# Laying out the first mixer's small operands and weights on the host instead of turning them on the chip

## The chip, the cores and the metric

The kernel runs on one core of a Trainium2 chip. The metric is the device time of one execution in microseconds, the median of several runs; lower is better. Arranging the input arrays on the host is not part of that time.

## What is computed

A block of two layers on 256 tokens of width 1024 (a conditioned mixer with a causal convolution, then a mixture of 32 experts, two per token), and behind it a second block of attention and feed-forward layers. The change touches the first block's mixers only, the first one above all:

```python
c_act = silu(c)
mods = (c_act @ ada_w[i] + ada_b[i])          # sh_m, sc_m, g_m, sh_f, sc_f, g_f
h = x * (1.0 + sc_m) + sh_m
# layer 0: conformer_conv
a, g = split(h @ w_in + b_in, 2)
u = a * sigmoid(g)
u = causal_depthwise_conv(u, w_dw) + b_dw     # 31 taps per channel
u = silu(layer_norm(u, ln_g, ln_b))
y = u @ w_out + b_out
# layer 1: short_gated_conv
gb, gc, v = split(h @ w_in, 3)
y = (gb * causal_depthwise_conv(gc * v, w_dw)) @ w_out    # 3 taps
# both: x = layer_norm(ALPHA * x + (1 + g_m) * y), then the mixture of experts
```

## The kernel before

The whole program is written under a manual schedule, each instruction with its engine: the text of the Python program is the order in which each engine gets its work.

**The stream of weights** (class `Stream`). All weights of both blocks go through one stream of units of up to 1 MB, loaded by SyncE (SP). There are 11 slots of 8 KB per partition, and 4 more lent during the first block. `pump` emits loads as long as slots are free, keeping one back; so the first `pump(0)`, inside `first_consts`, emits 14 units: `m` and `k` in the order m0 m1 k0 k1 m2 m3 k2 k3 m4 m5 k4 k5 m6 m7. Loads of later units are emitted where `done` or a split gives a slot back, so on SP they stand behind everything that was written before. Units of kind `k` and `i3` are split into two half-precision parts before use: ACT makes the high part (L120), VectorE the low one (L107). Behind k6 and k7 come i3 (two units), then a02 (four units for the modulation vectors g of layer 0), and so on to the experts.

**The start** (`first_consts`, L405). SP loads c, `ada_b`, x and then the units of `pump(0)`; behind them the 31 x 1024 tap matrix `wd` (L422), the rows `vq` and `vb`, and eight loads of the routers' weights and biases. TensorE turns `ada_b` (16 small transposes, L456 and L457) and x (16 transposes, L467, copied out by ACT, L468) so that channels lie on partitions. Two closures, `taps` and `vectors`, are kept for later.

**The first mixer's loop** (`first_mixer`, L711). For n = 0 to 3: `modulation(n)` multiplies two `m` units by c (L727), copies the result out as `adar` (L732), turns it (L735), sums it on VectorE into `c4` (L737), adds the bias `vb0` (L739), modulates two blocks of x (L574, L576, L580, L581: `mf`, `xh`, `xl`) and splits k(2n) and k(2n+1). Row block k multiplies one split unit by x (L752). The order is: the matmuls of `modulation(n)`, row block 2n-1 with the transposes of L735 inside, the rest of `modulation(n)`, for n = 2 `taps` and for n = 3 `vectors`, row block 2n; behind the loop the split of i3 and row block 7.

`taps` turns the 31 taps into what the convolution needs: 160 small matmuls (L478) and three transposes (L482) on TensorE, two copies on VectorE (`w4`, `taps`), and `m32`. `vectors` makes `vqT` (eight transposes, L495, one copy, L497), the scaled biases `ba` (L500, L501) and the routers' joined weights (L504, L505).

**The convolution.** Gates on ACT and VectorE use `vqT` and `ba`; GpSimd clears the borders of the tiles `U` (L787, L788) and builds diagonals from `m32` and `w4` (`diag`, L823); TensorE does five of eight channel blocks, VectorE the three in `VECTOR_Q` with `taps` as scalars (L795). M02 (L538) is the first step of that stage, product 6 (L777) the next.

Tiles of the pool `ch` (c8, `wd`, the routers' staging tiles, `c4`, `mf`) and of the pool `cv` (`sig`, `U`, `diag`, `V`) use the same memory one after the other; a tile of `cv` waits for the last reader of what lay there. Both blocks' later stages are not touched, except that layer 1's gated mixer takes its input weights and small vectors from the new arrays.

## Time and profile before

| | us |
|---|---|
| median of 3 runs (2452.61 to 2458.95) | 2457.27 |
| profiled execution, its own time | 2455.99 |
| span of the profiled execution | 2454.3 |
| TensorE busy | 2345.2 |
| VectorE busy | 1227.5 |
| ACT busy | 897.1 |
| GpSimd busy | 107.4 |

The span counts from the first to the last instruction. Instructions of one engine are listed with the line that issued them; L12 is line 12 of the kernel before. An idle time in square brackets is the time the engine stood still ahead of the instruction, with what ended it as far as the profile can tell; where an instruction waits for several things, the one named is the last by the profile's events, and can be a wrong one. Matmuls overlap, so the duration of a merged row of them counts from the first to the last. The TensorE clock is given as a share of the full rate. DMA rates are those of the core's 16 DMA engines together.

### The profile page before, as it was taken

What the parts mean: (1) busy time and instruction counts of PE and PEld (TensorE: products, weight loads), DVE (VectorE), ACT (ScalarE), POOL (GpSimd) and SP (SyncE); (2) the same over time, 40 slices, a digit from 0 to 9 for tenths busy, and PEclk for the clock granted to TensorE, in tenths of its full rate; (3) what the DMA queues carried; (4) which work ended last, traced back from release to release, by engine and by line L of the source; (5) the groups of instructions that cost most, each with busy time, mean ns of one, the idle gap of its engine ahead of it and who ended that gap; (6) DMA issues with size and microseconds to landing.
All of it is one profiled execution on the core that took longest, in us unless ns stands there. A gap on an engine that the chain in (4) does not pass through costs nothing.

```text
span 2454.3 us, 38061 instructions
## 1 busy us (share of the span) xinstructions
PE 2345.2 (96%) x16219; PEld 1383.2 (56%) x16219; DVE 1227.5 (50%) x1910; ACT 897.1 (37%) x1222; POOL 107.4 (4%) x169
## 2 busy tenths in 40 slices
PE   7989999999999999999979999999999999999998
PEld 5534343443386443334448855547888875554985
DVE  2775122111277222111157486968557567877654
ACT  2342111111143211111134447675444445676442
POOL 0100000000000000000020011110000002110000
PEclk8999999999999999999999999999999999999999
DMA  8977999999998999999976544536656555445651
GB/s 273 405 317 318 421 421 421 421 421 421 414 362 322 377 420 421 421 421 421 420 296 228 173 168 172 189 138 231 216 172 241 197 173 176 139 160 183 246 167 67
DMA packets 191033, 709.91 MB, mean 289 GB/s; under 512 B 15054, under 2 KB 50382, under 8 KB 134026
## 3 DMA queue, kind: packets, MB, share of 16 engines
q1 hardware_dynamic: 187850, 698.50, 73.7%
q10 hardware_dynamic: 3008, 8.92, 1.1%
q8 instruction: 129, 2.11, 0.3%
q14 instruction: 46, 0.38, 0.0%
HBM read 706.33 MB, written 1.05 MB: 288 GB/s over the span
## 4 chain that ended last, share of the span: by engine, by line
PE 50%; DMA 8%; issue 4%; DVE 4%; ACT 1%; POOL 0%; ACTq 0%; DVEq 0%; SPq 0%; POOLq 0%
PE ps L1470 18%; PE ps L1592 9%; PE ps L1198 6%; PE acc L1450 5%; DMA w<-in_e_w_up 3%; DMA w<-in_e_w_gate 3%; PE acc L1431 3%; PE ps L1220 2%; DVE w L107 1%; DMA w<-in_e_w_down 1%; PE acc L1692 1%; PE ps L1152 1%; PE ps L1954 1%; PE acc L1840 1%; PE acc L1236 1%
## 5 line engine op out<-in xcount | busy, mean ns | idle before, releaser
L107 DVE SCALAR_TENSOR_TENSOR w<-w,w 128x2048 f16<-128x2048 f32 (+3 forms) x239 | 525.6, 2213 | 234.8 <-ACT w L120 234.4
L120 ACT ACTIVATE w<-w 128x2048 f16<-128x2048 f32 (+3 forms) x239 | 434.6, 1832 | 251.5 <-PE ps L1470 140.0
L1470 PEld LDWEIGHTS <-w 128*128 128x128 f16 x4992 | 461.2, 112 | 11.4 <-issue 2.0
L1470 PE MATMUL ps<-xh,w 128*128 128x256 f16 (+1 forms) x3328 | 378.5, 257 | 1.1 <-DVE w L107 1.0
L1252 DVE SCALAR_TENSOR_TENSOR hid<-ps,ws,sil 128x512 f32<-128x512 f32 x32 | 24.0, 751 | 476.1 <-PE ps L1198 476.1
L1198 PE MATMUL ps<-w,xl 128*64 128x512 f32 x1024 | 240.4, 599 | 15.7 <-DMA w<-in_e_w_gate 15.6
L1198 PE MATMUL ps<-w,xh 128*64 128x512 f32 x1024 | 238.9, 595 | 14.8 <-DMA w<-in_e_w_gate 12.1
L1220 PE MATMUL ps<-w,hT 128*64 128x512 f32 x1024 | 237.0, 596 | 7.1 <-DMA w<-in_e_w_down 4.0
L1470 PE MATMUL ps<-xl,w 128*128 128x256 f16 (+1 forms) x1664 | 222.9, 257 | 1.9 <-DVE xl L333 1.9
L1592 PE MATMUL ps<-w,xh 128*128 128x512 f16 (+2 forms) x896 | 195.3, 362 | 0.5 <-ACT xh L332 0.5
L1198 PEld LDWEIGHTS ps<-w,xh 128*64 128x64 f32 x1024 | 80.0, 137 | 156.8 <-issue 121.2
L1198 PEld LDWEIGHTS ps<-w,xl 128*64 128x64 f32 x1024 | 78.4, 137 | 158.8 <-issue 120.1
L1220 PEld LDWEIGHTS ps<-w,hT 128*64 128x64 f32 x1024 | 80.3, 137 | 139.1 <-issue 111.0
L1227 ACT ACTIVATE yh<-y 128x512 f16<-128x512 f32 x64 | 40.3, 630 | 259.7 <-DVE y L1226 259.7
L1592 PEld LDWEIGHTS <-xh 128*128 128x128 f16 x896 | 85.4, 98 | 85.6 <-issue 2.4
L1226 DVE TENSOR_TENSOR y<-ps,g 128x512 f32<-128x512 f32 x64 | 44.0, 688 | 169.7 <-PE ps L1220 169.7
L1208 ACT ACTIVATE hT<-ps 128x512 f32<-128x512 f32 x32 | 19.1, 597 | 272.2 <-PE ps L1206 272.2
L1450 PE MATMUL acc<-w,hh 128*128 128x512 f16 x384 | 114.2, 379 | 0.0
L1592 PE MATMUL ps<-w,xl 128*128 128x512 f16 (+2 forms) x448 | 106.1, 362 | 0.0
L1431 PE MATMUL acc<-w,hh 128*128 128x512 f16 x320 | 95.2, 379 | 0.0
L1450 PE MATMUL acc<-w,hl 128*128 128x512 f16 x192 | 72.8, 379 | 0.0
L1592 PEld LDWEIGHTS <-xl 128*128 128x128 f16 x448 | 43.5, 98 | 45.7
(392 smaller groups left out, 2853.5 us busy)
## 6 DMA issues: line engine op xcount, KB each, us to landing
w<-in_e_w_gate SPq DMA_DIRECT2D x128, 1024.0 KB
w<-in_e_w_up SPq DMA_DIRECT2D x128, 1024.0 KB
w<-in_e_w_down SPq DMA_DIRECT2D x128, 1024.0 KB
w<-in_ffn_in SPq DMA_DIRECT2D x80, 1024.0 KB
w<-in_w_in SPq DMA_DIRECT2D x50, 1024.0 KB
w<-in_ffn_out SPq DMA_DIRECT2D x44, 1024.0 KB
w<-in_ada_w SPq DMA_DIRECT2D x40, 1024.0 KB
w<-in_b_w_in SPq DMA_DIRECT2D x12, 1024.0 KB
```

Of the source, the lines that this page charges most:

```text
L107: self.nc.vector.scalar_tensor_tensor(h[:, 1, :n], t[:, :n], WS, h[:, 0, :n], op0=OP.mult, op1=OP.subtract)
L120: self.nc.scalar.activation(h[:, 0, :n], t[:, :n], AF.Copy, scale=WS)
L1152: nc.tensor.matmul(pt[:, e * P : e * P + P], t[:, c, k + e :: 8], o[:, c], start=(i == c == 0), stop=(i == c == 1))
L1198: nc.tensor.matmul(pt[64 * e : 64 * e + 64], XT[j][:, 4 * h + k, 64 * e : 64 * e + 64], W[e][:, k * 512 : k * 512 + 512], start=(h == 0 an ...
L1220: nc.tensor.matmul(banks[n][64 * e : 64 * e + 64], hT[j][:, 2 * h + i, 64 * e : 64 * e + 64], W[e][:, i * D + n * 512 : i * D + n * 512 + ...
L1226: nc.vector.tensor_mul(y[:, sl], banks[n], G[:, sl])
L1227: nc.scalar.activation(yh[:, sl], y[:, sl], AF.Copy, scale=XS)
L1236: nc.tensor.matmul(accs[c][n], t, y[:, n * 512 : n * 512 + 512], start=False, stop=(j == 15 and i == 1), skip_group_check=True)
L1431: nc.tensor.matmul(accs[c][n], H[tx][:, 2 * h + f, c * P : c * P + P], ho[:, tw, f * D + n * 512 : f * D + n * 512 + 512], start=(j == 0 a ...
L1450: nc.tensor.matmul(accs[c][n], H[tx][:, 2 * h + f, c * P : c * P + P], ho[:, tw, f * D + n * 512 : f * D + n * 512 + 512], start=(j == 0 a ...
L1470: nc.tensor.matmul(pt[:, f % 2 * S + t0 : f % 2 * S + t1], h[:, tw, k * n + f : (k + 1) * n : nf], X[tx][:, 4 * (q % 2) + k, t0:t1], start ...
L1592: nc.tensor.matmul(pt[:, :n], X[tx][:, nk * q + k, c * P : c * P + P], h[:, tw, k * n : k * n + n], start=(q == 0 and k == 0 and tx == tw ...
```

## The change

Arrays are arranged on the host by `layouts` so that what one load brings lies in the order in which it is used: x by channel (`lay_x`), c with layer 0's two modulation biases (`lay_c`), one array per kind of unit in which each partition's part of a unit is contiguous (`lay_m`, `lay_k`, `lay_t` for i3, `lay_b` for layer 1's input weights), one array `lay_f` with `vbT`, `vqT`, `lnT` and the routers' weights side by side, and one, `lay_w`, with both forms of the taps. The transposes, the tap matmuls and the copies behind them are dropped; `taps` and `vectors` are no more. x by channel is loaded from ACT's queue; x by token is still loaded, behind the small rows. `ba` and `m32` are made at the end of `first_consts`.

The diff, with `first_units`' address arithmetic and the removed closures cut:

```diff
         def head(k):
             if k % 2 == 0:
-                src = a["ada_w"]
                 for h in range(2):
-                    m = [(dap(src, 4 * h * 6 * D + j * D + 128 * k, [[8 * 6 * D, P], [6 * D, 4], [1, 256]]), 256 * j, 256 * j + 256)
-                         for j in range(2)]
-                    u.setdefault("m", []).append(w.add(m, (4, 512), False))
-            u.setdefault("k", []).append(w.add([(dap(a["a_w_in"], 128 * k * 2 * D, [[2 * D, P], [D, 2], [1, 768]]), None, None)], (2, 768)))
+                    u.setdefault("m", []).append(block("lay_m", k + h, (4, 512), False))
+            u.setdefault("k", []).append(block("lay_k", k, (2, 768)))
...
+        def block(t, i, shape, split=True):
+            n = shape[0] * shape[1]
+            return w.add([(dap(a[t], i * P * n, [[n, P], [shape[1], shape[0]], [1, shape[1]]]), None, None)], shape, split)
...
     def first_consts(self, pool, early, keep, xT):
-        c8 = early.tile([P, 8], F32, name="c8")
-        vb = pool.tile([40, D], F32, name="vb")
-        vq = vb[32:]
-        wd = early.tile([31, D], F32, name="wd")
+        c8 = early.tile([P, 24], F32, name="c8")
+        vb = pool.tile([21, D], F32, name="vb")
+        fix = pool.tile([P, 768], F32, name="fix")
...
-        nc.sync.dma_start(c8, a["c"].rearrange("b (p k) -> p (b k)", p=P))
-        rows(nc.sync, vb[:12], self.ROWS_B[:1])
+        nc.sync.dma_start(c8, a["lay_c"])
+        nc.scalar.dma_start(xT, a["lay_x"])
+        self.w.pump(0)
+        t = keep.tile([P, 32 * 5 + 31 * 3], F32, name="taps")
+        nc.sync.dma_start(fix, a["lay_f"])
+        nc.sync.dma_start(t, a["lay_w"])
+        rows(nc.sync, vb, self.ROWS_B)
         nc.sync.dma_start(self.x, a["x"].rearrange("b (c p) d -> p (b c) d", p=P))
-        self.w.pump(0)
-        nc.sync.dma_start(wd, dap(a["a_w_dw"], 0, [[D, 31], [1, D]]))
-        rows(nc.sync, vq, self.ROWS_Q)
-        rows(nc.sync, vb[12:21], self.ROWS_B[1:])
         ca = self.ca = pool.tile([P, 8], F32, name="ca")
-        nc.scalar.activation(ca, c8, AF.Silu)
+        nc.scalar.activation(ca, c8[:, :8], AF.Silu)
+        self.w4 = t[:, : 32 * 5]
+        self.taps = {q: t[:, 160 + 31 * n : 191 + 31 * n] for n, q in enumerate(VECTOR_Q)}
+        self.vbT = fix[:, :96].rearrange("p (k r) -> p k r", k=8)
+        self.vqT = fix[:, 96:160].rearrange("p (k r) -> p k r", k=8)
+        self.lnT = fix[:, 160:192].rearrange("p (i l k) -> p i l k", i=2, l=2)
...
+            self.rw.append((fix[:, 192 + 288 * l : 480 + 288 * l].rearrange("p (k n) -> p k n", k=8), b))
...
         self.vb0 = pool.tile([P, 2, 8], F32, name="vb0")
         for j in range(2):
-            nc.vector.tensor_scalar(self.vb0[:, j], pt[:, 96 + j : 112 : 2], float(j), XS, op0=OP.add, op1=OP.mult)
+            nc.vector.tensor_scalar(self.vb0[:, j], c8[:, 8 + 8 * j : 16 + 8 * j], float(j), XS, op0=OP.add, op1=OP.mult)
...
+        m32 = self.m32 = keep.tile([P, 32], F32, name="m32")
+        nc.vector.tensor_reduce(m32, self.ident.rearrange("p (r j) -> p j r", r=4), axis=AX.X, op=OP.add)
+
+        self.ba = pool.tile([P, 8, 2], F32, name="ba")
+        for j in range(2):
+            nc.vector.tensor_scalar(self.ba[:, :, j], self.vqT[:, :, 2 * j], 1.0 / INV, None, op0=OP.mult)
...
     def first_mixer(self, pool, zp):
-                consts = list(self.first_consts(pool, mp, keep, z))
+                self.first_consts(pool, mp, keep, z)
...
                     next(m, None)
-                    if n > 1:
-                        consts.pop(0)(cb)
                     rows(2 * n)
```

`layouts` computes the arrays on the host by reshaping and transposing, for example:

```python
out["lay_x"] = v["x"][0].T.reshape(8, P, S).transpose(1, 0, 2)
w0 = v["ada_w"][0].reshape(P, 2, 4, 6, 4, 256)[:, :, :, :2]
out["lay_m"] = w0.transpose(4, 1, 0, 2, 3, 5)
wk = v["a_w_in"][0].reshape(8, P, 2, D)
out["lay_k"], out["lay_t"] = wk[..., :768], wk[..., 768:].transpose(2, 1, 0, 3)
```

## Rows read from the trace of the kernel before

**Rows 1.** The page, part 1: engine, busy us (share of the span), instructions.

```profile
PE 2345.2 (96%) x16219; PEld 1383.2 (56%) x16219; DVE 1227.5 (50%) x1910; ACT 897.1 (37%) x1222; POOL 107.4 (4%) x169
```

**Rows 2.** Stretches: length, busy us by engine (instructions), TensorE clock, DMA share, GB/s.

```profile
15.60:26.00 10.40, 6.01 (x37) 4.13 (x36) 4.96 (x6) 4.08 (x4) 0.00 (x0) 0.67 1.07 370
...
26.00:38.60 12.60, 10.69 (x97) 7.71 (x100) 4.96 (x6) 4.69 (x5) 0.00 (x0) 1.00 1.07 367
...
47.60:55.60 8.00, 7.95 (x161) 7.96 (x161) 1.76 (x1) 1.11 (x1) 0.00 (x0) 0.51 0.23 52
...
71.40:76.80 5.40, 5.37 (x34) 4.21 (x35) 2.71 (x8) 1.48 (x1) 1.08 (x3) 0.68 1.03 410
...
186.00:192.00 6.00, 6.00 (x42) 2.97 (x41) 4.04 (x16) 1.87 (x2) 0.00 (x0) 1.00 0.00 0
```

**Rows 3.** Order of time of SP's queue: start, duration, line, operation, count.

```profile
36.00 0.94 SPq L422 DMA_DIRECT2D wd<-in_a_w_dw  x1
...
52.80 4.50 SPq L93 DMA_DIRECT2D w<-in_a_w_in  x4
```

**Rows 4.** Order of time, TensorE's instructions: start, duration, line, operation, idle before.

```profile
13.20 1.06 PE L727 MATMUL ps<-w,ca 128*32 128x512 f32 x8 [1.60 <-DMA w<-in_ada_w]
...
26.03 1.92 PE L727 MATMUL ps<-w,ca 128*32 128x512 f32 x16
...
38.55 1.92 PE L727 MATMUL ps<-w,ca 128*32 128x512 f32 x16
...
47.65 8.00 PE L478 MATMUL ps<-ident,wd 31*32 31x8 f32 x160 [2.70 <-DMA wd<-in_a_w_dw]
...
62.72 1.92 PE L727 MATMUL ps<-w,ca 128*32 128x512 f32 x16
...
69.05 1.12 PE L495 MATMUL ps<-ident,vb 8*128 8x8 f32 x8
...
80.84 3.64 PE L538 MATMUL ps<-w,ca 128*32 128x512 f32 x32
...
86.48 0.27 PE L777 MATMUL ps<-xh,w 128*128 128x256 f16 x1 [2.00 <-DVE U L789]
```

**Rows 5.** Order of time, VectorE alone.

```profile
15.66 0.17 DVE L737 TENSOR_REDUCE c<-ps 128x4 f32<-128x16 f32 x1 [9.94 <-PE ps L735]
...
69.61 1.76 DVE L107 SCALAR_TENSOR_TENSOR w<-w,w 128x1536 f16<-128x1536 f32 x1 [0.68 <-ACT w L120]
...
72.92 1.76 DVE L107 SCALAR_TENSOR_TENSOR w<-w,w 128x1536 f16<-128x1536 f32 x1 [1.55 <-ACT w L120]
...
74.59 0.22 DVE L497 COPY vqT<-ps 128x64 f32<-128x64 f32 x1
...
78.96 2.81 DVE L107 SCALAR_TENSOR_TENSOR w<-w,w 128x2048 f16<-128x2048 f32 x1 [3.30 <-ACT w L120]
...
83.75 2.29 DVE L107 SCALAR_TENSOR_TENSOR w<-w,w 128x2048 f16<-128x2048 f32 x1 [1.98 <-ACT w L120]
```

**Rows 6.** Order of time, GpSimd alone.

```profile
68.99 0.13 POOL L787 MEMSET U<- 128x30 f32 x1 [12.62 <-DMA w<-in_ada_w]
...
75.72 0.12 POOL L787 MEMSET U<- 128x30 f32 x1 [6.29 <-DVE rw L505]
...
75.84 3.79 POOL L823 TENSOR_TENSOR diag<-m,w 128x1024 f32<-128x1024 f32 x2
```

**Rows 7.** DMA views: rate in 0.15 us slices (0:6), packets in 48:54, 300:312.

```profile
GB/s 0 0 0 0 0 0 0 0 0 0 0 0 12 15 1 164 164 0 55 109 27 0 55 0 27 328 273 355 382 437 437 328 382 410 437 437 382 437 437 437
...
DMA packets 1214, 0.36 MB, mean 59 GB/s; under 512 B 950, under 2 KB 1206, under 8 KB 1213
...
DMA packets 695, 5.06 MB, mean 422 GB/s; under 512 B 78, under 2 KB 78, under 8 KB 78
```

**Rows 8.** Waits of TensorE, 60 to 232 us, longest first: total, times, longest.

```profile
PE ps L556 <- DVE col L557: 4.8, 2, 2.5
```

**Rows 9.** Waits of all engines, 600 to 820 us: TensorE's longest for a load.

```profile
PEld ps L1220 <- DMA w<-in_e_w_down: 3.7, 3, 2.2
```

More of the change, by code (lines that the diff above doesn't have):

```diff
@@ L31 @@
 NEG = -1.0e30
+VECTOR_Q = (0, 2, 4)
 LOW = 2.0 ** 11
@@ L347 @@
     )
-    VECTOR_Q = (0, 2, 4)
     AFTER = ("F N G H", "S S F S N G S S")
@@ L386, in first_units @@
                 elif nm[0] == "i" and l == 0:
-                    u[nm] = [w.add([(dap(a["a_w_in"], j * D + 768, [[2 * D, P], [128 * 2 * D, 8], [1, 256]]), None, None)], (8, 256))
-                             for j in range(2)]
+                    u[nm] = [block("lay_t", j, (8, 256)) for j in range(2)]
                 elif nm[0] == "i":
-                    u[nm] = [cols(a["b_w_in"], 3 * D, j * D + 256 * int(nm[1]), nm != "i0") for j in (1, 2, 0)]
+                    u[nm] = [block("lay_b", 3 * int(nm[1]) + j, (8, 256), nm != "i0") for j in (1, 2, 0)]
                 elif nm == "o":
@@ L460, in first_consts @@
         for j in range(2):
-            nc.vector.tensor_scalar(self.vb0[:, j], pt[:, 96 + j : 112 : 2], float(j), XS, op0=OP.add, op1=OP.mult)
-        for k in range(0, 8, 2):
-            px = self.acc()
-            for e in range(2):
-                for c in range(2):
-                    o = e * S + c * P
-                    nc.tensor.transpose(px[:, o : o + P], self.x[:, c, (k + e) * P : (k + e) * P + P], self.ident)
-            nc.scalar.activation(xT[:, k : k + 2].rearrange("p k t -> p (k t)"), px, AF.Copy)
@@ L470, in taps @@
-        def taps(pt):
-            pq = [q for q in range(8) if q not in self.VECTOR_Q]
-            for r in range(4):
-                for n, q in enumerate(pq):
-                    for s in range(4):
-                        c0 = 256 * (q // 2) + 64 * s + q % 2
-                        nc.tensor.matmul(pt[32 * r : 32 * r + 32, (4 * n + s) * 8 : (4 * n + s) * 8 + 8], wd[:, c0 : c0 + 63 : 2],
-                                         self.ident[:31, r:32:4], start=True, stop=True, tile_position=(0, 32 * r))
-            for n, q in enumerate(self.VECTOR_Q):
-                c0 = 256 * (q // 2) + q % 2
-                nc.tensor.transpose(pt[:, 256 + 31 * n : 287 + 31 * n], wd[:, c0 : c0 + 255 : 2], self.ident[:31, :31])
-            w4 = self.w4 = keep.tile([P, 32 * len(pq)], F32, name="w4")
-            nc.vector.tensor_copy(w4, pt[:, : 32 * len(pq)])
-            t = keep.tile([P, 31 * len(self.VECTOR_Q)], F32, name="taps")
-            nc.vector.tensor_copy(t, pt[:, 256 : 256 + 31 * len(self.VECTOR_Q)])
-            self.taps = {q: t[:, 31 * n : 31 * n + 31] for n, q in enumerate(self.VECTOR_Q)}
-            m32 = self.m32 = keep.tile([P, 32], F32, name="m32")
-            nc.vector.tensor_reduce(m32, self.ident.rearrange("p (r j) -> p j r", r=4), axis=AX.X, op=OP.add)
@@ L818, in first_mixer @@
                     gate(q, out[q])
-                on = [q for q in range(8) if q not in self.VECTOR_Q]
+                on = [q for q in range(8) if q not in VECTOR_Q]
                 def diagonals(n):
@@ new lines, with layouts @@
+    "r_b_expert", "e_w_gate", "e_w_up", "e_w_down", "positions_2", "w_in_2", "sink_b_2", "w_br_a_2", "w_br_b_2", "w_br_c_2",
+    "w_out_2", "ffn1_in_2", "ffn1_out_2", "ffn2_in_2", "ffn2_out_2", "ln_g_2", "ln_b_2",
+    "lay_x", "lay_c", "lay_m", "lay_k", "lay_t", "lay_b", "lay_f", "lay_w",
+)
+def layouts(v):
+    out = {}
+    out["lay_x"] = v["x"][0].T.reshape(8, P, S).transpose(1, 0, 2)
+    b0 = v["ada_b"][0].reshape(6, 8, P)[:2].transpose(2, 0, 1).reshape(P, 16)
+    out["lay_c"] = np.concatenate([v["c"].reshape(P, 8), b0], axis=1)
+    w0 = v["ada_w"][0].reshape(P, 2, 4, 6, 4, 256)[:, :, :, :2]
+    out["lay_m"] = w0.transpose(4, 1, 0, 2, 3, 5)
+    wk = v["a_w_in"][0].reshape(8, P, 2, D)
+    out["lay_k"], out["lay_t"] = wk[..., :768], wk[..., 768:].transpose(2, 1, 0, 3)
+    out["lay_b"] = v["b_w_in"][0].reshape(P, 8, 3, 4, 256).transpose(3, 2, 0, 1, 4)
+    vb = v["ada_b"].reshape(12, P, 8).transpose(1, 2, 0)
+    rows = [v["a_b_in"].reshape(2, D)] + [v[n].reshape(-1, D) for n in ("a_b_dw", "a_ln_g", "a_ln_b", "b_w_dw")]
+    vq = np.concatenate(rows).reshape(8, 4, P, 2).transpose(2, 1, 3, 0)
+    ln = np.stack([v[n].reshape(2, P, 8) for n in ("mix_ln_g", "mix_ln_b")]).transpose(2, 0, 1, 3)
+    rw = [np.concatenate([v[f"r_w_{n}"][l].reshape(P, 8, -1) for n in ("group", "expert")], axis=2) for l in range(2)]
+    out["lay_f"] = np.concatenate([t.reshape(P, -1) for t in (vb, vq, ln, *rw)], axis=1)
+    wd = np.concatenate([v["a_w_dw"][0], np.zeros((1, D), np.float32)])
+    t = wd.reshape(8, 4, 4, 4, 32, 2).transpose(1, 4, 2, 5, 3, 0).reshape(P, 8, 32)
+    by = wd[:31].reshape(31, 4, P, 2).transpose(2, 1, 3, 0).reshape(P, 8, 31)
+    pq = [q for q in range(8) if q not in VECTOR_Q]
+    out["lay_w"] = np.concatenate([t[:, pq].reshape(P, -1), by[:, list(VECTOR_Q)].reshape(P, -1)], axis=1)
+    return {n: np.ascontiguousarray(t) for n, t in out.items()}
@@ L2005 @@
     arrays, aps = {}, {}
+    values = {n: np.ascontiguousarray(v) for n, v in inputs.items()}
+    values.update(layouts(values))
     for n in INS:
-        v = np.ascontiguousarray(inputs[n])
+        v = values[n]
         arrays[f"in_{n}"] = v
```

40 lines of the change are left out of this document (3 added, 37 removed).

## The prediction

> **What bounds the kernel now.** First the page: TensorE is busy for 96% of the span [rows 1], so time is lost or won only where TensorE stands still, runs at the lower of its two clocks (1.2 instead of 2.4 GHz), or does work that can go. Then the table of stretches [rows 2]: in the first 90 us there is one such place. From 47.6 to 55.6 us TensorE does 161 small tap operations at a granted clock of 0.51, and from 71.4 to 76.8 it has 0.68; between 26 and 38.6 the same loop ran at 1.00. Third, the order of time [rows 4]: the loop over n has its modulation matmuls (L727) at 13.20, 26.03, 38.55 and 62.72, and the next stage starts (L538) at 80.84. So the period from n=1 to 2 is 12.52 us, that from 2 to 3 is 24.17. The taps are in that one.
>
> What sets the ordinary period is a chain, not the stream of weights: adar, transposes, `c4` on VectorE (L737), modulate, split of `k` on ACT and VectorE, `rows`. In n=0 it starts with L737 at 15.66 [rows 5], and all that follows hangs on that instruction.
>
> **The order on each engine** decides this change. The kernel runs under a manual schedule. That VectorE keeps the written order is seen at 74.59 [rows 5]: the copy of `vqT` had its transposes complete at 70.17 [rows 4], VectorE stood idle from 71.37 to 72.92 between two splits, and still the copy ran only behind the second one, as written. SP does the same: the loads of k6 and k7 go out at 52.80 [rows 3], behind all the small ones, though m0's slot was free after the matmuls at 13.20 [rows 4].
>
> **Part 1: who waits for `fix`.** In the new code `fix` is loaded from SP behind `pump(0)`, that is behind the 14 units that fit the slots at once: 8 of `m` (1024 KB) and 6 of `k` (768 KB). `first_consts` now ends with the two `ba` operations on VectorE, which read `vqT` in `fix`. Before, they stood in the loop behind n=3's splits; now they stand ahead of the loop, so L737, L739, the modulations and every split queue behind them. Ahead of `fix`'s last byte pass 8 x 1024 + 6 x 768 KB, x (1024 KB, now on ACT's queue, beside them) and 384 KB of `fix`: 14,208 KB = 14.55 MB. The rate: the expert weights (8 KB in one piece per partition) run at 422 GB/s [rows 7]; the new units are one piece of 8 or 6 KB per partition, if the contiguous dimensions are merged. They are: in 48 to 54 us the four router loads went, which taken row by row would be 4 x 1024 packets, and the whole stretch has 1214 [rows 7]. So 34.5 us. Bytes flow at full rate from about 3.7 us now [rows 7]; with one small load fewer ahead I take 3.0. The last byte to its user: before, 3.2 MB (x, m0, m1, small ones) at 367 GB/s [rows 2] from 3.7 end at 12.4, and the second half of L727 starts at 13.20 [rows 4], so 0.8. Together 38.3; two `ba` of some 0.15 us make 38.6. L737 moves from 15.66 to 38.6: **+22.9 us**. Bounds: at the head's present 367 GB/s 39.6 instead of 34.5, so +28.0; from 2.5 us at the best slices' 437 GB/s [rows 7] +20.9. I take 422, since the pieces have that shape.
>
> The Trainium skill gives another rate: "DMA: Bandwidth & Descriptors", Where 436 GB/s comes from, says that HBM's share of about 358 GB/s binds for loads from HBM. By that the stream would take 40.6 us, an estimate, and this part would be +29.0. The 422 GB/s of this trace speak against it.
>
> What is dropped here (16 small and 16 large transposes, three VectorE operations, four ACT copies, all ahead of 13.20) would have brought the second half of `m` to some 11.1 us instead of 13.2, by (3.15 MB)/422 GB/s + 3.0 + 0.8. That gain of 2.1 us is gone behind the wait, since TensorE then has nothing to do until 38.6. Clock: n=0's `rows` run at the low clock before too (0.67 over 15.6 to 26 [rows 2]), so the long pause costs nothing further there.
>
> **Part 2: the taps go.** The 160 tap matmuls, three transposes, two copies and the wait for `wd` (issued at 36.00, 2.70 us of TensorE's wait [rows 3, 4]) leave n=2, and with them the low clock of the `rows` behind. n=2 then looks like n=1: 24.17 - 12.52 = **-11.65 us**. If its pauses still drop the clock, `rows` lose some 1.6 of it, as n=3's do (below).
>
> **Part 3: n=3.** The eight `vqT` transposes were covered by the wait for the split (69.05 to 70.17, split until 71.37 [rows 4, 5]), so they bring nothing themselves. But `rows` then ran at 0.68 of the clock: n=3 until L538 took 18.12 us, where 12.52 and the 4.0 of row block 7 (76.8 to 80.84) would be 16.5. So -1.6. The other side is GpSimd. Its two `diag` operations (3.79 us) ran at 75.84 [rows 6], because the memset at 75.72, ahead of them, waited for the memory of `rw`'s staging tiles. Those tiles are gone; what then lies last under the tiles `U` is `mf`, whose memsets ran at 68.99 [rows 6] (the row names a load; what ended just then is n=3's `xl` subtraction, the last reader of `mf`). Six pairs of memsets of some 0.1 us (75.72 to 75.84) put `diag` at about 69.58, and VectorE's split of k6 starts at 69.61 [rows 5]. The two do get in each other's way: the split at 78.96, beside the end of `diag`, took 2.81 us and the next, alone, 2.29 [rows 5]. Three outcomes, at the start of the next product (86.48 [rows 4]):
> - the split goes first: -1.6, and -0.5 since the split of i3 is undisturbed: -2.1;
> - `diag` goes first and the split comes between the two: `rows` start 1.9 later, behind a pause in which the clock drops, end at 78.7 instead of 76.8, minus 0.5: +1.4;
> - both `diag` go first: k6 is ready at 75.1, `rows` end at 80.5: +3.2.
>
> A difference of 30 ns is less than I can tell, so I take the middle of the first two, **-0.4**, and keep all three for the range.
>
> The Trainium skill, "SBUF — State Buffer", Who interferes with whom, says that a GpSimd operation reading SBUF and a VectorE operation with two SBUF inputs exclude each other for a whole instruction, whoever is first. By that the middle case costs `rows` 1.9 us, and the half microsecond lost at 78.96 agrees.
>
> **What costs nothing.** Stage by stage behind n=3: TensorE waits for no load from 60 to 232 us (first of 11 rows in [rows 8], none a DMA), and the stream ran empty at 186 to 192 us (0 GB/s [rows 2]), so loads follow TensorE there and a delay or gain passes whole into the experts, which start behind it with the same full slots. The second load of x (1 MB, 2.5 us of stream) stands ahead of k6; k6 lands near 46 us and is wanted near 80. `lay_b` makes layer 1's loads quicker (1 KB pieces now), but TensorE waits from 600 to 820 us for expert weights alone, 3.7 us the most [rows 9]. If that cover were gone, 12.6 MB at 422 instead of some 350 GB/s would bring 6 us. The router copies (4 on VectorE, under 1 us) stood in idle time.
>
> **Sum.** 22.9 - 11.65 - 0.4 = +10.85 us on the span of 2454.3, that is 2465.2; the profiled execution is 2455.99 with the 1.7 us around its span, and the median of the three runs lies 1.3 above that. On the median: 2457.3 + 10.8 = **2468.1 us**.
>
> **Rivals.**
> 1. *Faster: VectorE does not stand still*, since `fix` lands early. The mechanism: small transfers overtake the 1 MB ones. It breaks even when L737 runs 12.1 us late, with `fix` in hand at about 27.5 us. If it is there before 11 us: -2.1 - 11.65 - 2.1 = -15.85, 2441.4 us. Against it: `wd`, issued at 36.00 into a full queue, was waited for until 47.65 [rows 3, 4], when everything ahead had landed. Chance 0.12.
> 2. *The head's stream stays at 367 GB/s*, as a change that does not bring longer pieces: +28.0 - 11.65 - 0.4 = +15.95, 2473.2 us. For it: a stream from two queues is not seen at 422. Chance 0.11.
> 3. *The delay is made good later*: while VectorE stands, SP has loaded k6 and k7, and the experts of layer 0 wait for loads. If the stream stayed ahead, up to all 10.8 would come back: 2457 us. Against it the empty stream at 186 us. Chance 0.07.
>
> **How the numbers follow.** The forecast (+8.5 to +14.5: 2465.8 to 2471.8, with the three outcomes of part 3) has 0.70, the rivals 0.12, 0.11 and 0.07. The range 2463 to 2474 takes in the forecast and rival 2 and leaves out the ends of the first and third; it holds 0.81. About 0.3% (7.4 us) is what a measurement of this kernel can tell from no change. Slower by more than that: nearly all of the forecast and rival 2, 0.79. Within: the third rival and the forecast's low end, 0.09. Faster: 0.12.
>
> **What would show it.** Right: VectorE idle from about 3 to 38 us, released by the load of `fix`, with `ba` and then L737 behind it at 38 to 39; TensorE idle from about 14 to 41; L727 at 49, 61.5 and 74; no low clock behind 62; `diag` beside the splits of n=3. Wrong: L737 before 20 us, which is rival 1; `fix` later than 42, rival 2; L538 some 10 us late and the experts of layer 0 ending less late than they started, rival 3. The prediction falls most simply if `fix` lands at another time than 38 us.

## The result: slower by 0.74%, and the profile after

| | before | after |
|---|---|---|
| time, us (median; lowest to highest; runs) | 2455.36 (2452.61 to 2458.95; 4) | 2473.69 (2472.77 to 2475.24; 4) |
| profiled execution, us (its span) | 2455.99 (2454.3) | 2474.0 (2472.3) |
| ratio, after to before | | 1.0074, 95% interval 1.0057 to 1.0092 |

The change makes the kernel slower by 18 us; 10.85 were forecast. Lines have moved: in the kernel after, L689 is the old L737 (`c4`), L679 the old L727 (modulation), L704 the old L752 (`rows`), L109 and L122 the old L107 and L120 (split on VectorE and ACT), L508 the old L556, L754 the old L804, L762 the old L812, L490 the old L538, L739 the old L789 (`U`), L773 the old L823 (`diag`). GpSimd's memsets, the old L787 and L788, are now L737 and L738; they have nothing to do with the old L737.

The page, part 1, of the kernel after, beside [rows 1]:

```profile
PE 2333.4 (94%) x16016; PEld 1372.1 (55%) x16016; DVE 1227.4 (50%) x1902; ACT 894.8 (36%) x1218; POOL 108.5 (4%) x169
```

TensorE has 12 us less to do and the kernel is 18 us longer: the loss is time in which TensorE stands or is slow. The table of stretches, beside [rows 2] (length; PE, PEld, DVE, ACT, POOL busy and instructions; clock; DMA share; GB/s):

```profile
15.60:38.00 22.40, 0.00 (x0) 0.00 (x0) 0.08 (x1) 0.00 (x0) 0.00 (x0) 1.00 1.00 412
38.00:51.80 13.80, 9.44 (x60) 5.71 (x61) 5.03 (x8) 4.68 (x5) 0.00 (x0) 1.00 0.79 286
51.80:66.00 14.20, 12.28 (x95) 8.53 (x93) 4.96 (x6) 4.69 (x5) 0.00 (x0) 0.88 0.80 295
66.00:78.50 12.50, 10.58 (x95) 7.62 (x93) 4.96 (x6) 4.69 (x5) 0.00 (x0) 1.00 0.53 199
82.70:92.60 9.90, 6.71 (x34) 4.67 (x35) 5.32 (x2) 1.49 (x2) 5.48 (x8) 0.66 0.66 237
```

From 15.6 to 38 us the compute engines stand (VectorE has 0.08 us), while the DMA runs at 412 GB/s. The stretch with the taps is gone. The clock of 1.00 in the first two rows, and in the two rows of the head under e6, is no reading: these traces have no entry of the clock before 47.8 us (52.4 in e6), and the view then shows 1.00. By their pace the matmuls of n=0 run at the low clock until 47.6 us (0.42 us apiece in `rows`, 0.27 behind that), and in e3, which has the same wait, the entry is there: 0.50 from 15.6 to 46 us. VectorE in order of time, beside [rows 5]:

```profile
37.92 0.25 DVE L460 TENSOR_SCALAR ba<-fix 128x8 f32<-128x8 f32 x2 [31.51 <-DMA fix<-in_lay_f]
38.08 0.17 DVE L689 TENSOR_REDUCE c<-ps 128x4 f32<-128x16 f32 x1
```

VectorE stood 31.51 us for `fix`, and L689 comes at 38.08 instead of 15.66. TensorE's modulations and transposes, beside [rows 4]:

```profile
49.13 1.06 PE L679 MATMUL ps<-w,ca 128*32 128x512 f32 x8
...
52.31 0.60 PE L687 MATMUL ps<-ident,adar 128*128 128x128 f32 x4
...
63.33 1.06 PE L679 MATMUL ps<-w,ca 128*32 128x512 f32 x8
...
66.50 0.60 PE L687 MATMUL ps<-ident,adar 128*128 128x128 f32 x4
...
75.85 1.06 PE L679 MATMUL ps<-w,ca 128*32 128x512 f32 x8
```

The period from n=2 to 3 is 12.52 us as forecast, but the one from n=1 to 2 is 14.20 (12.52 before). In n=3, VectorE and GpSimd, beside [rows 5, 6]:

```profile
79.66 0.17 DVE L689 TENSOR_REDUCE c<-ps 128x4 f32<-128x16 f32 x1 [4.38 <-PE ps L687]
...
82.74 3.48 DVE L109 SCALAR_TENSOR_TENSOR w<-w,w 128x1536 f16<-128x1536 f32 x1 [0.68 <-DMA w<-in_ada_w]
87.78 1.83 DVE L109 SCALAR_TENSOR_TENSOR w<-w,w 128x1536 f16<-128x1536 f32 x1 [1.55 <-ACT w L122]
95.02 2.29 DVE L109 SCALAR_TENSOR_TENSOR w<-w,w 128x2048 f16<-128x2048 f32 x1 [5.41 <-ACT w L122]
...
101.50 0.87 DVE L739 SCALAR_TENSOR_TENSOR U<-ps,ba,sig 128x256 f32<-128x256 f32 x2
```

```profile
82.12 0.13 POOL L737 MEMSET U<- 128x30 f32 x1 [79.32 <-DVE xl L533]
...
82.70 5.30 POOL L773 TENSOR_TENSOR diag<-m,taps 128x1024 f32<-128x1024 f32 x2
```

GpSimd's memsets now wait for `xl`, `diag` starts 40 ns ahead of the split, and the split takes 3.48 instead of 1.76 us. (Its row names a load; what ended just then, at 82.71, is ACT's half of the split.) `rows` go on behind that split, before and after:

```profile
71.43 0.39 PE L752 MATMUL acc<-xh,w 128*128 128x256 f16 x2 [0.93 <-DVE w L107]
```

```profile
86.29 0.61 PE L704 MATMUL acc<-xh,w 128*128 128x256 f16 x2 [3.13 <-DVE w L109]
```

**The ledger by stage.** All profiles can be cut at the same instructions: `c4` of n=0 to 3 (L689), the first `U`, the first batch statistics behind the convolution, the 14th group of `hid` transposes in layer 0's experts (608.79 us before), the end. Lengths in us, worked out from start times; names are those of the experiments below:

| kernel | `c4` of n=0 at | n=0 | n=1 | n=2 | n=3 to U | U to statistics | to 14th `hid` | to the end |
|---|---|---|---|---|---|---|---|---|
| before | 15.66 | 14.18 | 12.52 | 24.18 | 19.41 | 75.01 | 447.8 | 1845.5 |
| after | 38.08 | 14.87 | 14.19 | 12.52 | 21.84 | 76.72 | 448.9 | 1845.2 |
| e1 | 13.90 | 14.20 | 12.52 | 14.19 | 21.48 | 76.54 | 447.9 | 1846.1 |
| e2 | 15.69 | 14.24 | 12.52 | 14.20 | 21.51 | 76.55 | 448.0 | 1845.9 |
| e3 | 38.13 | 14.09 | 12.53 | 14.19 | 18.88 | 77.77 | 446.4 | 1843.5 |
| e4 | 14.05 | 14.24 | 12.52 | 14.19 | 18.90 | 78.47 | 446.1 | 1845.0 |
| e6 | 43.07 | 14.66 | 14.18 | 12.52 | 21.73 | 76.68 | 448.7 | 1843.6 |
| e7 | 15.29 | 13.98 | 12.53 | 14.19 | 18.08 | 78.77 | 446.5 | 1845.3 |
| e8 | 13.64 | 12.53 | 12.53 | 12.52 | 17.34 | 76.68 | 447.4 | 1844.4 |
| e9 | 12.29 | 14.12 | 12.52 | 14.19 | 18.90 | 77.77 | 448.1 | 1846.4 |
| e10 | 13.71 | 12.52 | 12.52 | 12.53 | 17.35 | 85.40 | 445.7 | 1845.2 |
| e11 | 11.63 | 12.62 | 12.52 | 12.53 | 17.34 | 86.24 | 447.2 | 1843.4 |
| e12 | 11.38 | 13.01 | 12.52 | 12.53 | 17.34 | 75.00 | 447.6 | 1844.7 |
| e13 | 38.53 | 15.10 | 12.52 | 12.52 | 17.35 | 76.52 | 447.3 | 1849.1 |

After against before: +22.42 +0.69 +1.67 -11.66 +2.43 +1.71 +1.06 -0.32 = +18.0 us.

### The profile page after: what moved, and what is told of

It is laid out like the page before. It is cut to its first block, busy times and chain, and to the rows that moved or that the text cites. A ratio compares the mean times of both kernels' runs of the same rounds, so it can differ in the third digit from the quotient of the medians.

```text
span 2472.3 us, 37610 instructions
## 1 busy us (share of the span) xinstructions
PE 2333.4 (94%) x16016; PEld 1372.1 (55%) x16016; DVE 1227.4 (50%) x1902; ACT 894.8 (36%) x1218; POOL 108.5 (4%) x169
## 4 chain that ended last, share of the span: by engine, by line
PE 48%; DMA 11%; issue 3%; DVE 3%; ACT 1%; POOL 0%; ACTq 0%; SPq 0%; DVEq 0%; POOLq 0%
PE ps L1420 18%; PE ps L1542 9%; PE acc L1400 5%; PE ps L1148 4%; PE acc L1381 4%; DMA w<-in_e_w_up 4%; DMA w<-in_e_w_gate 4%; DMA w<-in_e_w_down 2%; PE ps L1170 2%; DVE w L109 1%; PE acc L1642 1%; PE ps L1904 1%; PE acc L1790 1%; PE acc L1880 1%; PE ps L1887 1%
## 5 line engine op out<-in xcount | busy, mean ns | idle before, releaser
L109 DVE SCALAR_TENSOR_TENSOR w<-w,w 128x2048 f16<-128x2048 f32 (+3 forms) x239 | 526.8, 2219 | 239.5 <-ACT w L122 238.5
L122 ACT ACTIVATE w<-w 128x2048 f16<-128x2048 f32 (+3 forms) x239 | 434.7, 1832 | 254.9 <-PE ps L1420 141.1
L1148 PE MATMUL ps<-w,xl 128*64 128x512 f32 x1024 | 240.0, 599 | 15.6 <-DMA w<-in_e_w_gate 15.6
```

What stands on the lines that cost most here:

```text
L109: self.nc.vector.scalar_tensor_tensor(h[:, 1, :n], t[:, :n], WS, h[:, 0, :n], op0=OP.mult, op1=OP.subtract)
L122: self.nc.scalar.activation(h[:, 0, :n], t[:, :n], AF.Copy, scale=WS)
L1148: nc.tensor.matmul(pt[64 * e : 64 * e + 64], XT[j][:, 4 * h + k, 64 * e : 64 * e + 64], W[e][:, k * 512 : k * 512 + 512], start=(h == 0 an ...
```

## The experiments

The times are medians. The ratios are to the kernel before, run on the same chip. Its median there was 2455.8 us for e1 to e4, 2454.1 for e6 to e9, 2454.7 for e10 and e11 and 2454.2 for e12 and e13; where runs from different chips are compared, the distance of each to its own kernel before is given.

**e1: `ba` back behind the splits.**

```
-        for j in range(2):                        # first_consts
-            nc.vector.tensor_scalar(self.ba[:, :, j], ...)
                     next(m, None)
+                    if n == 3:
+                        for j in range(2):
+                            nc.vector.tensor_scalar(self.ba[:, :, j], ...)
```

> The changed kernel with one edit: the two `ba` operations on VectorE stand behind n=3's splits again, as in the kernel before; `fix` is loaded where the change put it. Theory A (VectorE's written order makes all of the first stage wait for `fix`): L689 moves from 38.08 us to about 13.5 (15.66 before, less the 2.1 us by which the second half of `m` is in hand sooner), and the lower clock in n=0 and n=1 costs no more than before. Sum against the kernel before: -2.1 - 11.65 (taps) + 2.4 (n=3 with `diag` beside the splits, as read in the changed kernel) = -11.35, so 2444 us; 2446.8 if the 1.7 us at the pause in the convolution and the 1.05 us in the experts come again. Theory B (the stream of weights sets the pace of the first stage anyway, since k6 and k7 land at about 46 us): L689 early, but TensorE waits for loads at n=2 and n=3, and the time is 2455 to 2470 us. Theory C (the delay of VectorE is made good later, so nothing is won by undoing it): 2470 us or more.

Measured: 2448.2 us, ratio 0.9971 (0.9961 to 0.9980). VectorE in order of time:

```profile
6.07 0.36 DVE L456 TENSOR_REDUCE m<-ident 128x32 f32<-128x128 f32 x1
13.90 0.17 DVE L687 TENSOR_REDUCE c<-ps 128x4 f32<-128x16 f32 x1 [7.47 <-PE ps L685]
```

L687, the old L737, comes 24.2 us sooner than in the kernel after, and the whole kernel ends 25.5 us sooner. Nothing else was edited, so the wait was VectorE's order, theory A. B and C fall. What then remains is a gain of 7 to 8 us instead of the 11.35 written down: n=2 takes 14.19 instead of 12.52, and the stretch from U to the statistics 76.54 instead of 75.01. Both were named with the expectation or in the prediction as what could come on top.

**e2: `fix` ahead of the weights.**

```
         nc.sync.dma_start(c8, a["lay_c"])
+        nc.sync.dma_start(fix, a["lay_f"])
         nc.scalar.dma_start(xT, a["lay_x"])
         self.w.pump(0)
-        nc.sync.dma_start(fix, a["lay_f"])
```

> The changed kernel with the load of `fix` (384 KB) issued on SP directly behind `c8`, ahead of the weights; `ba` stays ahead of the loop. Theory A (the wait is the meeting of an early reader and a late load, and either cure does): L689 at about 14.5 us, 0.9 us behind the run with late `ba` (384 KB at 422 GB/s), so 2445 us, or 2447.7 with the two later costs. Theory B (small pieces of `fix` are slow wherever they stand, or something else than this load holds VectorE): L689 stays above 25 us and the time above 2460 us.

Measured: 2449.8 us, ratio 0.9978 (0.9968 to 0.9987).

```profile
6.83 0.25 DVE L460 TENSOR_SCALAR ba<-fix 128x8 f32<-128x8 f32 x2 [0.37 <-DMA fix<-in_lay_f]
15.69 0.17 DVE L689 TENSOR_REDUCE c<-ps 128x4 f32<-128x16 f32 x1 [8.61 <-PE ps L687]
```

The same `ba` at the same place now waits 0.37 us. Either cure does: the loss was the meeting of an early reader and a late load. The detour of 384 KB costs L689 1.8 us against e1. Of these, 1.06 are the loads: the first modulation starts at 9.42 instead of 8.36 us, about the 0.93 us that its bytes take at 422 GB/s. The rest is TensorE's pace, with 1.93 instead of 1.67 us for the second half of the modulation and 1.08 instead of 0.63 for the transposes behind it. The median is 1.6 us above e1's.

**e3: `diag` spaced, `ba` as changed.**

```
-        nc.vector.tensor_reduce(m32, self.ident..., op=OP.add)       # first_consts
+        for i in range(2):                                           # in place of the split of the two k units
+            w.split(u["k"][2 * n + i])
+            if n == 3:
+                nc.vector.tensor_reduce(self.m32[i], self.ident..., op=OP.add)
```

> The changed kernel with `ba` where it is, but with GpSimd's two `diag` operations released one behind each split of n=3: `m32` is computed twice on VectorE, behind the split of k6 and behind that of k7, and each `diag` reads its own copy. Theory A (the 2.4 us that n=3 loses come from `diag` and the split of k6 taking turns, 5.30 and 3.48 us instead of 3.79 and 1.76): the split of k6 takes about 1.76 us, U starts 2.4 us sooner, 2471.3 us. Theory B (the loss is the low clock of `rows` behind a pause that is there anyway): the splits are quick again, but U moves by less than 0.8 us, 2473 us or more. Theory C (`diag` fits no gap and only moves its collision to the split of k7 or to i3): U starts at most 0.5 us sooner or later.

Measured: 2470.1 us, ratio 1.0064 (1.0047 to 1.0081). VectorE, then GpSimd:

```profile
82.02 1.76 DVE L109 SCALAR_TENSOR_TENSOR w<-w,w 128x1536 f16<-128x1536 f32 x1 [0.68 <-ACT w L122]
83.69 0.37 DVE L696 TENSOR_REDUCE m<-ident 128x32 f32<-128x128 f32 x1
85.32 2.35 DVE L109 SCALAR_TENSOR_TENSOR w<-w,w 128x1536 f16<-128x1536 f32 x1 [1.26 <-ACT w L122]
```

```profile
84.14 1.91 POOL L775 TENSOR_TENSOR diag<-m,taps 128x1024 f32<-128x1024 f32 x1 [2.13 <-DVE m L696]
88.03 1.91 POOL L775 TENSOR_TENSOR diag<-m,taps 128x1024 f32<-128x1024 f32 x1 [1.98 <-DVE m L696]
```

Alone, one `diag` takes 1.91 us and the split 1.76. The way from n=3's `c4` to U falls from 21.84 to 18.88: 2.96 us, theory A (2.4 expected). The second split still meets the end of the first `diag` (86.05) and is 0.6 us longer for it.

**e4: both edits.** The diffs of e1 and e3 together.

> Both edits together: `ba` behind n=3's splits and `diag` released one behind each split. If both mechanisms are as told and independent: 2.4 us below the run with late `ba` alone, so 2441.6 to 2444.4 us, which is 0.45 to 0.56% below the kernel before. If `diag`'s collision is not what n=3 loses: the same time as with late `ba` alone.

Measured: 2447.1 us, ratio 0.9965 (0.9954 to 0.9977). From n=3's `c4` to U 18.90 instead of 21.48 in e1: 2.58, as expected. But the median is only 1.1 below e1's. In the profile 1.9 of the gain go again between U and the statistics (78.47), and 1.8 come back by the 14th `hid` (446.1 against 447.9); the runs lie between 2444.1 and 2450.3 us. How much of the local gain reaches the end is not shown.

**e6: the weights of the first mixer from the original tensors.** The `m` and `k` units are loaded by the lines of the kernel before; `lay_m` and `lay_k` are gone.

```
-                    u.setdefault("m", []).append(block("lay_m", k + h, (4, 512), False))
-            u.setdefault("k", []).append(block("lay_k", k, (2, 768)))
+                    m = [(dap(a["ada_w"], 4 * h * 6 * D + j * D + 128 * k, [[8 * 6 * D, P], [6 * D, 4], [1, 256]]), 256 * j, 256 * j + 256)
+                         for j in range(2)]
+                    u.setdefault("m", []).append(w.add(m, (4, 512), False))
+            u.setdefault("k", []).append(w.add([(dap(a["a_w_in"], 128 * k * 2 * D, [[2 * D, P], [D, 2], [1, 768]]), None, None)], (2, 768)))
```

> The changed kernel, but the `m` and `k` units of the first mixer are read from the original tensors again (pieces of 1 KB and 3 KB instead of 8 and 6 KB); all else as changed. Theory A (the prediction's: the head's stream runs at 422 GB/s because its pieces are long, and at 367 with the old ones): the 14.55 MB ahead of `fix`'s user take 39.6 instead of 34.5 us, L689 moves from 38.08 to about 43.2, the time from 2473.7 to about 2479. Theory B (the piece length doesn't matter at these sizes; the old head was slow for another reason, its small loads): L689 within 1 us of 38.1, 2473 to 2475 us.

Measured: 2477.1 us, ratio 1.0092 (1.0075 to 1.0109). The same 30 us of the head, first in the kernel after, then in e6 (last column GB/s):

```profile
4.00:34.00 30.00, 4.96 (x20) 1.14 (x20) 0.51 (x3) 0.81 (x2) 0.00 (x0) 1.00 1.01 421
```

```profile
4.00:34.00 30.00, 4.95 (x20) 1.18 (x20) 0.51 (x3) 0.81 (x2) 0.00 (x0) 1.00 1.07 371
```

421 against 371 GB/s, where the prediction had 422 and 367; the matching L691 at 43.07, 4.99 us later, where 5.1 were expected. Theory A. So of the layouts, those of `m` and `k` are worth 5 us under this wait. At the end of the program 3.4 of them are left by the medians, 4.6 by the distance to the kernel before.

**e7: the taps alone.** The kernel before; `wd`'s load is replaced by one of `lay_w`, and the tap matmuls, three transposes and two copies are gone.

```
-        wd = early.tile([31, D], F32, name="wd")
+        tw = keep.tile([P, 32 * 5 + 31 * 3], F32, name="taps")
...
-        nc.sync.dma_start(wd, dap(a["a_w_dw"], 0, [[D, 31], [1, D]]))
+        nc.sync.dma_start(tw, a["lay_w"])
...
         def taps(pt):
-            for r in range(4):
...
             m32 = self.m32 = keep.tile([P, 32], F32, name="m32")
```

> The kernel before with one part of the change: the taps come laid out by unit from the host (one load in the place of `wd`), the 160 tap matmuls, three transposes and two copies are gone; everything else is as before. Theory A (the prediction's part 2: n=2 then looks like n=1, 12.52 us): -11.65, that is 2443.7 us. Theory B (the pauses of the loop still drop the clock once, as in all four profiles without the taps, where one period took 14.19 us): -10.0, 2445.4 us, and 2447 if the pause in the convolution then also falls on the low clock, as it did in those profiles. Theory C (the tap matmuls stood beside other waits and their going frees little): 2450 us or more.

Measured: 2446.4 us, ratio 0.9975 (0.9964 to 0.9985). n=2 takes 14.19 us instead of 24.18: -9.99, theory B; from U to the statistics it loses 3.8 us again. In n=3 `diag` starts at 65.81 us, behind both splits (59.07 and 62.38), and the way from `c4` to U is 18.08 us, 1.33 less than before: most of the 1.6 that the prediction gave to the clock there, without the collision.

**e8: unread matmuls in the pauses of the first stage.** The edit is shown against e4; the unread matmuls are called fillers below.

```
+                def fill(count):
+                    for _ in range(count):
+                        nc.tensor.matmul(mb[:, :P], self.ident, self.ident, start=True, stop=True)
+                fill(24)
                 for n in range(4):
...
                     next(m, None)
+                    fill(10 if n else 20)
```

> The version with late `ba` and spaced `diag`, plus matmuls of the identity whose result nobody reads (24 before n=0's modulation, 20 before its `rows`, 10 before the `rows` of n=1 to 3), so that TensorE has no pause of over 1 us in the first stage. Theory A (what the loop loses against 12.52 us a period is TensorE's clock, which falls behind the pauses): granted clock 1.00 from the first modulation on, modulations at 1.06 instead of 1.94 us, periods of 12.5 instead of 14.2 us at n=0 and at n=2, U 3 to 4 us sooner, about 2443.5 us. Theory B (the periods are set by the splits on ACT and VectorE, and the clock is hidden behind them): periods and time unchanged or up to 1 us longer, 2447 to 2448 us.

Measured: 2439.9 us, ratio 0.9948 (0.9931 to 0.9964). Four stretches of 12.5 us from n=0 to 3:

```profile
13.00:25.50 12.50, 12.25 (x108) 9.82 (x109) 4.96 (x6) 4.69 (x5) 0.00 (x0) 1.00 1.02 421
25.50:38.00 12.50, 12.50 (x114) 9.95 (x113) 4.96 (x6) 4.69 (x5) 0.00 (x0) 1.00 1.00 410
38.00:50.50 12.50, 12.50 (x115) 9.96 (x113) 4.96 (x6) 4.68 (x5) 0.00 (x0) 1.00 0.72 276
50.50:63.00 12.50, 12.50 (x117) 11.30 (x115) 7.31 (x11) 6.00 (x5) 4.63 (x18) 1.00 1.02 414
```

Granted clock 1.00 throughout, every period 12.5 us, U 5.3 us sooner than in e4. The kernel is 7.2 us faster by the medians, and 5.6 by the distance to the kernel before (14.2 against 8.7). Theory A, and more than expected: the lower clock cost 1.71 at n=0, 1.67 at n=2 and 1.56 at n=3. What TensorE does in a pause is useless work, and it pays.

**e9: x behind the first two `m` units.** The edit is shown against e4.

```
-        nc.scalar.dma_start(xT, a["lay_x"])
+        for _ in range(2):
+            self.w._load()
+        nc.sync.dma_start(xT, a["lay_x"])
         self.w.pump(0)
```

> The version with late `ba` and spaced `diag`, with the load of the transposed x (1 MB) issued on SP behind the first two `m` units instead of on ACT's queue beside them. Theory A (the first modulation waits for bytes: x shares the stream with the first two units): `c8` lands before 4 us, the first modulation starts at about 6 instead of 8.4 us and L689 at about 11.5 instead of 14.05, 2.5 us less, 2444.6 us. Theory B (the first landing is set by the latency of the queue, or x is then what the modulate waits for): L689 or the modulate behind it stays where it is, 2447 us.

Measured: 2446.0 us, ratio 0.9967 (0.9953 to 0.9981). `c8` is in hand at 2.46 instead of 5.97 us, the first modulation starts at 6.89 instead of 8.39, `c4` at 12.29 instead of 14.05: theory A, with 1.8 instead of 2.5 us. At the end nothing of it can be seen: the median is 1.1 us below e4's, and 8.1 below the kernel before, where e4 was 8.7 (runs from 2441.6 to 2447.8).

**e10 and e11: unread matmuls in the convolution too.** The fillers of e8 also ahead of the two groups of transposes that wait for VectorE's column sums; e11 also has e9's edit.

```
             t = self.col[l, j] = self.gp.tile([P, 8], F32, name=f"col{l}{j}")
+            more = {(0, 4): 14, (1, 1): 24}.get((l, j), 0)
+            if more:
+                f = self.acc()
+                for _ in range(more):
+                    nc.tensor.matmul(f[:, :P], self.ident, self.ident, start=True, stop=True)
```

> The version with matmuls that nobody reads in the first stage, and more of them (14 and 24) ahead of the two groups of transposes in the convolution that wait 2.5 and 4.1 us for VectorE's column sums. Theory A (the 1.7 us between U and the batch statistics, 76.7 instead of 75.0 us, are TensorE's lower clock behind these two pauses): granted clock 1.00 there, 75.0 us or less from U to the statistics, 2438.2 us. Theory B (VectorE, busy without a gap over those 59 us, sets the pace and TensorE's clock is hidden behind it): the clock is 1.00 and the stretch stays at 76.7 us, 2439.9 us.

> The same with the load of x behind the first two `m` units (and 18 instead of 24 matmuls ahead of n=0's modulation). If the stages add up: L689 at about 11.9 us instead of 13.64, another 1.8 us less, 2436.4 to 2438.1 us, which is 0.75% below the kernel before. If the experts' loads have become the bound by then (the stream of weights, not TensorE, decides when layer 0's experts end): the first stage is 1.8 us shorter and the experts start sooner, but end where they did, 2438 to 2440 us.

Measured: 2450.1 us (0.9985, 0.9976 to 0.9995) and 2448.7 us (0.9973, 0.9963 to 0.9982), against 2439.9 without. TensorE in e10:

```profile
116.10 3.66 PE L776 MATMUL ps<-V,diag 128*32 128x256 f32 x64
119.58 1.03 PE L487 MATMUL ps<-w,ca 128*32 128x512 f32 x4
127.47 5.02 PE L487 MATMUL ps<-w,ca 128*32 128x512 f32 x28 [6.87 <-DVE col L511]
132.42 5.62 PE L506 MATMUL acc<-ident 128*128 128x128 f32 x48
```

The modulation matmuls (L487), which in e8 ran through before the pause, now wait 6.87 us for the very column sum that was to be bridged, so the fillers come behind it and VectorE's next splits 8 us late; U to the statistics takes 85.40 us. Why the matmuls have this wait here and not in e8 (another PSUM bank given out would do it) was not settled. Neither theory of e10 is tested by this run, and none of e11's, whose first stage is as short as expected (`c4` at 11.63) but whose convolution has the same wait (86.24 us).

**e12: the best of it.** e8 with e9's edit and 14 instead of 24 fillers at the start; nothing in the convolution.

> The version with late `ba`, spaced `diag` and unread matmuls in the first stage only (none in the convolution), with the load of x behind the first two `m` units and 14 matmuls ahead of n=0's modulation. If the stages add up: L689 at 11.6 to 12.0 us instead of 13.64, so 1.8 us below 2439.9: 2438 us, 0.7% below the kernel before. If the experts' loads are the bound by then: the experts' first product is 1.8 us sooner and their last one where it was, 2439.5 to 2440.5 us.

Measured: 2438.2 us, ratio 0.9936 (0.9919 to 0.9953), 16 us below the kernel before, where the changed one is 18 above it. `c4` comes at 11.38 us and U 1.78 us sooner than in e8; the stages add up. The stretch from U to the statistics is another 1.68 us shorter than in e8, which the median does not show (1.7 below e8's in all; runs from 2435.8 to 2440.1). By chance e12 also settles what e10 could not. TensorE in the convolution of the kernel before, of the kernel after, and of e12:

```profile
132.87 5.35 PE L812 MATMUL ps<-V,diag 128*32 128x256 f32 x64
144.72 1.13 PE L556 MATMUL ps<-ident,adar 128*128 128x128 f32 x8 [2.29 <-DVE col L557]
```

```profile
147.36 1.13 PE L508 MATMUL ps<-ident,adar 128*128 128x128 f32 x8 [2.53 <-DVE col L509]
148.42 3.66 PE L762 MATMUL ps<-V,diag 128*32 128x256 f32 x64
151.90 4.41 PE L490 MATMUL ps<-w,ca 128*32 128x512 f32 x32
160.41 1.94 PE L508 MATMUL ps<-ident,adar 128*128 128x128 f32 x8 [4.11 <-DVE col L509]
162.28 2.88 PE L754 MATMUL acc<-U,ident 128*32 128x284 f32 x32
```

```profile
112.64 1.13 PE L507 MATMUL ps<-ident,adar 128*128 128x128 f32 x8 [2.51 <-DVE col L508]
113.70 5.35 PE L773 MATMUL ps<-V,diag 128*32 128x256 f32 x64
118.86 4.41 PE L489 MATMUL ps<-w,ca 128*32 128x512 f32 x32
125.55 1.13 PE L507 MATMUL ps<-ident,adar 128*128 128x128 f32 x8 [2.28 <-DVE col L508]
126.61 2.12 PE L765 MATMUL acc<-U,ident 128*32 128x284 f32 x32
```

In e12, as in the kernel before, the clock falls behind the first pause: the product with `diag` takes 5.35 instead of 3.66 us, and the next wait for VectorE takes that up. In the kernel after it falls behind the second: transposes and shift take 1.94 and 2.88 instead of 1.13 and 2.12 us, with nothing behind to absorb it, and the stretch is 1.7 us longer.

All profiles without fillers in the convolution sort in this way, by the granted clock over the 8 us from U + 45 (behind the first pause) and the 9 us from U + 57 (behind the second). It is 0.79 and 1.00 in the kernel before and e12, with 75.0 us from U to the statistics; 1.00 and 0.81 in the kernel after, e1, e2, e6, e8 and e13, with 76.5 to 76.7; 1.00 and 0.62 in e3 and e9, with 77.8; and 0.79 and 0.81 in e4 and e7, whose clock also falls in the first 14 us behind U, with 78.5 and 78.8. e8 and e12 run the same program from U on. What decides behind which pause the clock falls is not shown.

**e13: the wait kept, the rest cured.** The kernel after with e3's edit and e8's fillers (without the 24 at the start).

> The changed kernel with its wait for `fix` kept, but with the two things taken out that the prediction had too small: `diag` released one behind each split, and unread matmuls (20 before n=0's `rows`, 10 before those of n=1 to 3) against the pauses of the first stage. Theory A (the prediction's wait was right, and what it lacked in the first stage is `diag`'s collision and TensorE's clock): L689 at 38.1 us as in the changed kernel, periods of 12.5 us, U at 38.1 + 54.9 = 93.0 instead of 101.5 us (54.9 as in the run with the fillers and late `ba`), 8.5 us below the changed kernel, 2465.2 us. Theory B (behind a pause of 24 us other things are late as well, loads or the queue): U later than 96 us, and the time above 2468 us.

Measured: 2470.6 us, ratio 1.0062 (1.0045 to 1.0079). The periods of n=1 and n=2 are 12.52 us and n=3 takes 17.35 to U, as with late `ba`; but n=0 takes 15.10, not 12.5, since the 20 fillers end at 20.9 and TensorE then stands 20.72 us. So U comes at 96.02: 5.5 of the 8.5 us. By the numbers written down that is theory B, U later than 96 and the time above 2468, though what is late is neither a load nor the queue but n=0 at the low clock (`rows` at 0.42 us a matmul until 48.5). The end shows 3.1 us by the medians and 2.0 by the distance to the kernel before; in the profile the stages behind the experts took 1849.1 us, 2.7 more than in any other of the table.

## Why the prediction was right, and where its sum was short

**Right: the sign, and the mechanism of part 1. In the range by luck.** The measured 2473.7 us lie outside the forecast's own 2465.8 to 2471.8 and inside the range of 2463 to 2474 by 0.3 us; the range reaches so far only to take in rival 2, and rival 2 did not happen. Of the signs named for being right, VectorE's idle time, `ba` and L689 at 38, TensorE's idle time until 41.17 and `diag` beside the splits came. The modulations came at 49.13, 63.33 and 75.85 instead of 49, 61.5 and 74, and "no low clock behind 62" is false: from 82.7 to 92.6 us it is 0.66.

The mechanism came as told. L689 moved by 22.42 us, where 22.9 were summed: the stream ran at 421 GB/s (422 taken), `fix` was used at 37.92 (38.3), and with the old pieces the rate fell to 371 (367). e1 and e2 each take the wait away by another end. Rival 1 is out: the small load did not overtake the large ones (issued at 21.3, landed 16.6 us later). Rival 2 had 2473.2 us, by accident nearly the time measured; the head's rate rules it out. Rival 3 is out: the delay grew from 15.55 us at U to 18.3 at the 14th `hid`, and was not made good. The rate of "DMA: Bandwidth & Descriptors" in the Trainium skill (Where 436 GB/s comes from, 358 GB/s for loads from HBM) is not what binds here: 421 GB/s over 30 us.

**Short: the sum, 10.85 forecast against 18.0 of span.** The 7.15 us are these steps:

- *Part 1's clock sentence* ("costs nothing further there"): +0.69 in n=0. In e3, with the same pause, n=0 took 14.09 us, no more than before; there the matmuls of `rows` reach the full pace at 46.4 us, in the kernel after at 47.6, with `c4` at the same time. So the sentence holds within about 0.7 us; what it missed is that n=0 runs at the low clock with or without the pause, and that this is worth 1.7 us (e8).
- *Part 2*, mis-sized: "n=2 then looks like n=1" gave -11.65. The case in its last sentence ("if its pauses still drop the clock") is what happened, in all profiles without the taps and without fillers: one of n=1 and n=2 takes 14.19 us. So the taps are worth -9.99 (e7). In the kernel after the low clock fell into n=1 and left n=2 at a clean 12.52, and the two errors of place cancel: -11.66 + 1.67 = -9.99.
- *Part 3*, mis-sized: -0.4 was a middle of two cases, +2.43 was measured. What happened is the case "`diag` goes first and the split comes between", summed at +1.4. Counted from `c4`, `rows` go on behind the split 1.74 us later than before (1.9 taken), and 0.50 come back by U (0.5 taken). What the case left out is that `rows` themselves take longer: 6.58 us at a clock of 0.55 (86.3 to 92.9) instead of 5.39 at 0.68 (71.4 to 76.8 [rows 2]), 1.19 more. The step that failed is the middle: the choice hung on 30 ns, and the two orders should have stood as two forecasts. Spacing `diag` takes away 2.6 to 3.0 us (e1 to e4, after to e3).
- *"What costs nothing"*, wrong: the delay does not pass unchanged. From U to the statistics +1.71, since the clock falls at a pause without slack behind it instead of one with slack (after against e12). To the 14th `hid` another +1.06: TensorE reaches the experts 16.23 us late, is 16.87 late at their eighth group, 18.25 at the ninth and 18.32 at the 14th, in the stretch where it waits for loads (13.7 us in 12 waits before, 15.0 in 13 after). That the loads themselves were so late is concluded from these waits, not read.
- *Head*: -2.1 was said to be there for whoever does not wait. By its own terms the sum gives 11.3 us and -1.9, not 11.1 and -2.1 (and the lower bound of part 1 +21.2 with `ba` counted, not +20.9). With late `ba` it is -1.76 (e1), though the second half of the modulation starts already at 10.74: without the 32 transposes ahead of it TensorE starts at the low pace, and that half takes 1.67 instead of 1.06 us.

Two waits belong to the experts' term (the view of waits: who waited for what, in total, times, longest). SP's small transfers of the router ahead of the experts, before and after:

```profile
SPq L1050 <- SPq L1050: 6.3, 4, 2.5
```

```profile
SPq L1000 <- SPq L1000: 8.9, 5, 3.2
```

And TensorE in the experts of layer 0, a wait that the kernel before did not have there:

```profile
PE ps L1170 <- DMA w<-in_e_w_down: 1.0, 1, 1.0
```

SP waits 2.6 us longer for itself just where the stream of the experts' weights restarts. Why was not tried, and that this is the 1.06 us is not shown. `lay_b` alone was not tried either.

So the 7.15 us are 2.83 in n=3 (1.19 of it the clock's), 4.06 of clock elsewhere (n=0 0.69, n=1 1.66, convolution 1.71), 1.06 in the experts, less 0.48 of part 1 and 0.32 at the end. The last column of the ledger differs by up to 5.7 us from profile to profile without any edit there, and the one to the 14th `hid` by 3.2 (445.7 to 448.9), so the 1.06 us, and every term below it, are no more than this one profile's. The clock stood in the argument as a bonus of 1.6 in two places; it should have stood in the range as a loss at every pause that stays.
